# The start of a hybrid attention layer put in another order: modulation weights first, then the first head on half of the input

## The chip, the cores and the metric

The kernel runs on one core of a Trainium2 chip. The metric is the device time of one execution in microseconds (us). Five engines work beside each other, each through its own queue in order: TensorE (PE, matmuls; PEld is its weight load), VectorE (DVE), ScalarE (ACT), GpSimd (POOL) and SyncE (SP, which here issues every DMA).

## The reference

One layer of a diffusion backbone, for 1024 latent tokens and 256 context tokens of 1024 channels, in float32. What matters here is how it starts:

```python
shift_x, scale_x, gate_x = jnp.split(jax.nn.silu(c) @ w_mod[l] + b_mod[l], 3, axis=-1)
shift_c, scale_c, gate_c = jnp.split(jax.nn.silu(c_ctx) @ w_mod[l] + b_mod[l], 3, axis=-1)
hc = rmsnorm(ctx, norm_g[l]) * (1.0 + scale_c) + shift_c
...
_, s_f, s_b = gla_bidir(qc, kc, vc, laf_c, lab_c, s_zero, s_zero, not last)
hx = rmsnorm(x, norm_g[l]) * (1.0 + scale_x) + shift_x
q, k, v, la_f, la_b, zA, uB, zB, gA, gB = mixer_inputs(hx, w_in[l], ...)
ox, _, _ = gla_bidir(q, k, v, la_f, la_b, s_f, s_b, True)
```

The conditioning vectors give a shift and a scale for every channel. Each token row is normalised, scaled and shifted; that gives `h`. Then `h` is multiplied by the columns of `w_in`: queries, keys (4 heads of 128) and values (4 heads of 256), low-rank decay inputs, and the columns of the pooling branch and of the gates. The context gives the start states of the latent scans of all heads, so the gated linear attention of the first head waits for the context.

## The kernel before

**Numbers.** Every projection works on split floats: a float32 value is written as a high part (rounded to the matmul's `fp32r` format, by ScalarE) and a low part (the difference, by VectorE). `split` issues these two instructions. A product is then three `fp32r` matmuls (high·high, high·low, low·high), as in `proj_t` and `proj_n`.

**Modulation.** The loop over `b` in 0..3 (lines 211 to 243) makes shift and scale for both halves of the channels: b=0 is the shift of channels 0 to 511, b=1 their scale, b=2 and b=3 the same for channels 512 to 1023. For each it loads eight 256 KB pieces of `w_mod`. Pieces with an even index are multiplied as plain float32 (one `matmul` of the program, two on the engine); pieces with an odd index are split and multiplied as two `fp32r` matmuls. The stationary operand has only 4 columns. Then `mrow`, four small transposes (line 233) and two or three VectorE instructions give `shA` and `sA`.

**Token rows.** `load_x` and `normalise` bring in ten tiles of 128 tokens: tiles 0 and 1 are the context, 2 to 5 the first latent half, 6 to 9 the second. `split_rows` (line 184) takes one of eight channel blocks `kt` of a half: four transposes into a PSUM bank (`psc` for even kt, `ppj` for odd), then ScalarE and VectorE apply scale and shift and write the high and low part (`hH`, `hL`). `latent_rows(g, kts)` does this for latent half g, `context_rows` for the context. Channel blocks 0 to 3 need b=0 and b=1 only, blocks 4 to 7 need b=2 and b=3.

**Order.** Program order is: modulation b=0, b=1 with tiles 2 to 5 in between; `latent_rows(0, 0..3)`; low-rank weights (eight small loads for `wup`); modulation b=2, b=3 with tiles 0, 1, 6, 7, 8 in between, then tile 9; masks and rope tables; `latent_rows(0, 4..7)`; `low_rank(1)`; `context_rows`; `low_rank(0)`; `latent_rows(1)`; `low_rank(2)`; `ctx_gates` (decays of the context, all heads); and then the first head: `head_k`, `ctx_k`, `head_q`, `gates(0)`, `head_v`, `ctx_state(0)`. After these come the context states of heads 1 to 3 and `gla` for head 0. The rest (three more heads, pooling branch, gates, output) follows and is not touched.

**What sets the real order.** The program names tiles by a tag; a tag has a fixed number of buffers (`BUFS`, and `BANKS` for PSUM), and a new tile waits until the oldest one of its tag is released. A scheduler at build time lays out each engine's queue: it takes program order as the priority and may let an instruction that is ready pass one that waits. SP issues DMAs in its queue's order, and a load whose buffer isn't free holds up all that are behind it. Tags that matter here: `h` (32 buffers, modulation weights and then hH, hL), `wr` (2, raw weights), `wh`/`wl` (4 each, split weights), `bx` (1), `sw` (2), `pj` (3 banks), `sc` (2 banks), `tr`, `st` and `o` (1 bank each). `ctx_gates` and `gates` both use `bx`; `gates` and `ctx_state` both use the bank `tr`.

Of the kernel before, what the change touches and what calls it, by code (L numbers as in the profile page):

```python
# [10 lines left out]
F32R = mybir.dt.float32r  # L11
# [4 lines left out]
P = 128  # L16
D = 1024
KT = D // P
# [25 lines left out]
def hybrid_kernel(ctx: ExitStack, tc: tile.TileContext, x, ctx_in, rows, w_mod, b_gate_row,  # L44
# [83 lines left out]
    def load_x(t):  # L128
        tag = "S0" if t < 2 else "v" if t < 6 else "qk"
        loaded.append(t)  # L130
        src = ctx_in[t * P:(t + 1) * P] if t < 2 else x[(t - 2) * P:(t - 1) * P]
        xs[t] = [T(tag, [P, HALF]) for dh in range(2)]
        for dh in range(2):
            load(xs[t][dh], src[:, dh * HALF:(dh + 1) * HALF])
# [11 lines left out]
    def low_rank_weights():  # L146
        wraw = T("wr", [P, KT, 32])
        load(wraw, w_in[:, O_LR:O_LR + 32].rearrange("(k p) n -> p k n", p=P))
# [3 lines left out]
        for d in range(2):  # L152
            for part, srcw in enumerate((wlh, wll)):
                for rep in range(2):
                    act(wlr[:, :, d, part, rep, :], srcw[:, :, d * 16:(d + 1) * 16].bitcast(F32))
        wup = T("wr", [P, HALF])
        for rep in range(4):
            load(wup[rep * 16:(rep + 1) * 16], w_up_f)
            load(wup[64 + rep * 16:64 + (rep + 1) * 16], w_up_b)
        wup_hi, wup_lo = T("lr", [P, HALF], F32R), T("lr", [P, HALF], F32R)  # L160
# [23 lines left out]
    def split_rows(kt, t0, n, c, hi, lo):  # L184
        pt, sc_c, sh_c = modulate(kt, t0, n, c, ("sc", "pj")[kt % 2])
        hf = T("s2", [P, n])
# [21 lines left out]

    token_tiles = [2, 3, 4, 5, 0, 1, 6, 7, 8, 9]
    loaded = []  # L210
    for b in range(4):
        s_, half_ = b % 2, b // 2
        c0 = s_ * D + half_ * HALF
        pm = PT("st" if b % 2 else "tr")
        if b == 2:
            wlr, wup_hi, wup_lo = low_rank_weights()
        for kt in range(KT):
            w = T("h", [P, HALF])
            load(w, w_mod[kt * P:(kt + 1) * P, c0:c0 + HALF])
            if kt % 2 == 1 and token_tiles and b * KT + kt in (1, 3, 5, 7, 17, 19, 21, 23, 25, 27):  # L220
                load_x(token_tiles.pop(0))
                normalise(loaded[-1])
            if kt % 2 == 0:
# [5 lines left out]
            mm(pm[:4], cs4[:, kt, :], lo, False, kt == KT - 1)  # L229
        mrow = T("on", [4, HALF])  # L230
        act(mrow, pm[:4])
# [12 lines left out]

        if b == 1:
            latent_rows(0, range(4))
    for t in token_tiles:
        load_x(t)
    for t in token_tiles:
        normalise(t)  # L250

# [163 lines left out]

    def head_v(h, st):
        wv = weights_v(h)
        for t in range(8):
            if t % 2 == 0:
# [197 lines left out]

    msk_f = T("bx", [P, len(LEVELS) - 1, HC])
    load(msk_f, masks)
    nc.vector.tensor_copy(msk, msk_f)  # L620
    rope_t = T("t8", [P, 2, L])
    load(rope_t, rope)
    cosT, sinT = rope_t[:, 0, :], rope_t[:, 1, :]
    latent_rows(0, range(4, KT))
# [12 lines left out]
    ctx_state(0, kc, ctx_v(wv))  # L637
# [502 lines left out]
```

## Time and profile before

| | |
|---|---|
| median of 3 runs | 1144.55 us (1141.5 to 1146.18) |
| the profiled execution | 1143.17 us, of which the span is 1141.4 us |
| granted TensorE clock, mean | 0.996 |
| busy share of the span | PE 97%, PEld 79%, DVE 69%, ACT 44% |
| bytes moved | 138.21 MB, mean 121 GB/s |

The time of the profiled execution is its span and 1.8 us around it. Times in the rows are microseconds from the start of the span. A busy TensorE is one that has matmuls under way: since they are pipelined, it can count as busy while it waits inside a group, so the distance between starts says more than the length. The granted clock is a share of full speed: 1.00 is the level of 2.4 GHz, 0.5 that of 1.2 GHz, and a value between is a mean over the stretch.

### The profile page before, as it was taken

Reading aid. Unit: us, or ns where it says so; the run is one execution under the profiler, and the core shown is the slowest. Engines: PE = TensorE matmul, PEld = TensorE weight load, DVE = VectorE, ACT = ScalarE, POOL = GpSimd, SP = SyncE. Lnnn points to the kernel's source line nnn. Section 1 sums busy time; section 2 is a strip of 40 time slices with the busy share of each in tenths; the row PEclk is TensorE's granted clock in tenths of the full one; section 3 lists DMA queues with packets and bytes.
Section 4 is the critical chain, followed back from the end, with each engine's and each line's share of the span. In section 5 each row is a group of like instructions: output and inputs, shape, how many; then the busy total and the mean of one; then the engine's idle time right before and its main releaser. Section 6 shows DMA issues by size and latency. Waiting matters only on the chain.

```text
span 1141.4 us, 17328 instructions
## 1 busy us (share of the span) xinstructions
PE 1107.9 (97%) x6505; PEld 900.8 (79%) x6505; DVE 787.6 (69%) x1498; ACT 506.7 (44%) x994; POOL 25.5 (2%) x50
## 2 busy tenths in 40 slices
PE   6799999999999999999999999999999999999997
PEld 1268997797797787788888878888887787878997
DVE  4677458477487486798988977665657886647454
ACT  6687554464554543543333533343346422114233
POOL 0100000100100100100000000000000000000001
PEclk9899999999999999999999999999999999999999
DMA  8812150220210310113251664523239568962113
GB/s 293 286 38 74 50 150 24 63 67 20 76 55 20 93 38 20 56 31 121 97 162 42 203 194 129 162 84 126 91 122 313 199 194 304 307 222 93 38 38 148
DMA packets 119665, 138.21 MB, mean 121 GB/s; under 512 B 8803, under 2 KB 80797, under 8 KB 119454
## 3 DMA queue, kind: packets, MB, share of 16 engines
q1 hardware_dynamic: 119582, 137.12, 37.4%
q8 instruction: 51, 0.84, 0.3%
q14 instruction: 32, 0.26, 0.1%
HBM read 100.38 MB, written 32.51 MB: 116 GB/s over the span
## 4 chain that ended last, share of the span: by engine, by line
PE 85%; DMA 5%; ACT 4%; issue 2%; DVE 2%; SPq 1%; POOL 1%; POOLq 0%; ACTq 0%; DVEq 0%
PE ppj L78 60%; PE psc L78 17%; PE pst L78 3%; PE po L78 2%; PE ptr L78 2%; DMA h<-w_mod 1%; SPq L81 1%; ACT A L64 1%; POOL r L611 1%; ACT sw L64 1%; PE ptr L363 1%; DMA h<-ga 1%; DMA wr<-w_in 0%; ACT h L64 0%; DMA kt<-ga 0%
## 5 line engine op out<-in xcount | busy, mean ns | idle before, releaser
L78 PE MATMUL ppj<-h,wh 128*128 128x512 f32 x794 | 266.9, 404 | 1.1 <-DVE h L67 1.1
L64 ACT ACTIVATE wh<-wr 128x512 fp32r<-128x512 f32 (+1 forms) x183 | 113.8, 628 | 175.3 <-PE ppj L78 104.9
L78 PEld LDWEIGHTS ppj<-h,wh 128*128 128x128 f32 x794 | 148.0, 188 | 36.2 <-issue 2.0
L67 DVE TENSOR_TENSOR wl<-wr,wh 128x512 fp32r<-128x512 f32 (+1 forms) x183 | 124.4, 685 | 67.3 <-ACT wh L64 66.3
L78 PE MATMUL ppj<-wh,h 128*128 128x256 f32 x800 | 157.7, 283 | 0.0
L78 PE MATMUL ppj<-h,wl 128*128 128x512 f32 x397 | 157.1, 396 | 0.0
L78 PEld LDWEIGHTS ppj<-wh,h 128*128 128x128 f32 x800 | 130.5, 192 | 0.6 <-ACT qk L64 0.4
L78 PE MATMUL ppj<-wl,h 128*128 128x256 f32 x400 | 113.1, 283 | 0.0
L78 PEld LDWEIGHTS ppj<-h,wl 128*128 128x128 f32 x397 | 74.6, 188 | 15.2 <-issue 1.0
L78 PEld LDWEIGHTS ppj<-wl,h 128*128 128x128 f32 x400 | 76.6, 192 | 0.3 <-DVE wl L67 0.2
L75 DVE SCALAR_TENSOR_TENSOR S<-S,dec,pst 128x256 f32<-128x256 f32 x56 | 26.8, 479 | 42.5 <-PE pst L78 42.2
L64 ACT ACTIVATE s<-s 128x512 f32<-128x512 f32 x60 | 36.9, 629 | 35.8 <-DVE s L67 32.6
L67 DVE TENSOR_TENSOR s<-s,ppj 128x512 f32<-128x512 f32 x60 | 40.6, 681 | 15.5 <-PE ppj L78 15.5
L64 ACT ACTIVATE s<-qk 128x256 f32<-128x256 f32 x56 | 23.3, 425 | 47.4 <-DVE qk L67 47.3
L78 PE MATMUL ppj<-S,wh 128*128 128x512 f32 (+1 forms) x132 | 40.9, 371 | 0.0
L67 DVE TENSOR_TENSOR s<-s,psc 128x512 f32<-128x512 f32 x43 | 29.2, 682 | 16.0 <-PE psc L78 16.0
L78 PEld LDWEIGHTS psc<-z,s 128*64 128x64 f32 x768 | 26.4, 136 | 17.4 <-issue 14.5
L78 PE MATMUL psc<-h,wh 128*128 128x512 f32 x126 | 39.1, 392 | 0.0
L78 PE MATMUL pst<-v,kt 128*128 128x256 f32 x112 | 35.6, 399 | 0.0
L78 PE MATMUL ppj<-v,wh 128*128 128x512 f32 (+1 forms) x116 | 35.0, 360 | 0.0
L67 DVE TENSOR_TENSOR s<-s,bx 128x256 f32<-128x256 f32 (+1 forms) x64 | 30.3, 483 | 6.7 <-ACT bx L64 6.7
L64 ACT ACTIVATE qk<-wr 128x512 fp32r<-128x512 f32 x30 | 18.4, 626 | 35.9 <-DVE wr L67 21.2
(513 smaller groups left out, 2361.7 us busy)
## 6 DMA issues: line engine op xcount, KB each, us to landing
wr<-w_in SPq DMA_DIRECT2D x65, 512.0 KB, 3.7
h<-w_mod SPq DMA_DIRECT2D x32, 256.0 KB, 5.4
qk<-sg SPq DMA_DIRECT2D x32, 256.0 KB, 5.6
sg<-s SPq DMA_DIRECT2D x28, 256.0 KB, 2.1
sw<-qk SPq DMA_DIRECT2D x64, 64.0 KB, 2.0
gb_T<-qk SPq DMA_DIRECT2D x16, 256.0 KB, 2.8
qk<-o SPq DMA_DIRECT2D x16, 256.0 KB, 4.9
ga<-s SPq DMA_DIRECT2D x16, 256.0 KB, 3.9
```

The lines of the kernel that those rows point to most:

```text
L64: return nc.scalar.activation(out, in_, func, **kw)
L67: return nc.vector.tensor_tensor(out=out, in0=a, in1=b, op=op)
L75: return nc.vector.scalar_tensor_tensor(out=out, in0=a, scalar=s, in1=b, op0=op0, op1=op1)
L78: return nc.tensor.matmul(out, lhsT=lhsT, rhs=rhs, start=start, stop=stop)
L81: return nc.sync.dma_start(out=out, in_=in_)
L363: nc.tensor.transpose(pt[:, i * P:(i + 1) * P], src[i], ident)
L611: nc.gpsimd.tensor_tensor(out=r2[:, 2, :], in0=r2[:, 1, :], in1=mhalf.to_broadcast([P, 2]), op=ALU.pow)
```

## The change

The start is written in another order, and some of its parts change size or place.

- Modulation b=0 and b=1: six of eight pieces are now multiplied as plain float32 and two are split (before four and four). Tiles 2 to 5 are still loaded in between, at other places. b=2 and b=3 keep four and four.
- The key weights of head 0 are loaded right behind b=1, then the pieces of b=2, the query weights, and the pieces of b=3. The key weights get a tile `kbig` of tag `bx` for their split parts, the query weights four tiles of tag `s2`.
- Then follow the products of b=2 and b=3, the first half of the contraction of K and Q for token half 0 (`proj_part` with channel blocks 0 to 3), the low-rank weights, the loads of the context tiles and of tiles 6 to 9, `latent_rows(0, 4..7)`, the rest of K and Q for half 0, the loads of V's weights, rope and masks, the rotation of K and Q, the context tiles' norms, V for half 0, `context_rows`, `low_rank(1)`, the norms of tiles 6 to 9, `low_rank(0)`, `latent_rows(1)`, `ctx_k`, K for half 1, `low_rank(2)`, `ctx_gates`, Q for half 1, `gates(0)`, V for half 1, and `ctx_state(0)` as before.
- `split_rows` uses the two `sc` banks alone. The low-rank weights' raw tile goes to tag `A`, `wup` to `sw` and is loaded by two broadcast DMAs; tiles 6 to 9 go to `kt`, `qk`, `qk` and `S`; the masks' raw tile goes to `on`.

```diff
     def load_x(t):
-        tag = "S0" if t < 2 else "v" if t < 6 else "qk"
-        loaded.append(t)
+        tag = "S0" if t < 2 else "v" if t < 6 else ("kt", "qk", "qk", "S")[t - 6]
...
-        wup = T("wr", [P, HALF])
-        for rep in range(4):
-            load(wup[rep * 16:(rep + 1) * 16], w_up_f)
-            load(wup[64 + rep * 16:64 + (rep + 1) * 16], w_up_b)
+        wup = T("sw", [P, HALF])
+        for d, src in enumerate((w_up_f, w_up_b)):
+            load(wup[64 * d:64 * d + 64],
+                 src.rearrange("(a r) n -> a r n", a=1).to_broadcast([4, 16, HALF]))
...
-        pt, sc_c, sh_c = modulate(kt, t0, n, c, ("sc", "pj")[kt % 2])
+        pt, sc_c, sh_c = modulate(kt, t0, n, c, "sc")
...
+    def mod_part(b, pm, ws, kts):
+        for w, kt in zip(ws, kts):
+            if kt % (4, 2)[b // 2] != (3, 1)[b // 2]:
                 mm(pm[:4], sil4[:, kt, :], w, kt == 0, kt == KT - 1)
                 continue
             hi, lo = T("wh", [P, HALF], F32R), T("wl", [P, HALF], F32R)
             split(hi, lo, w)
             mm(pm[:4], cs4[:, kt, :], hi, kt == 0, False)
             mm(pm[:4], cs4[:, kt, :], lo, False, kt == KT - 1)
...
+    x_after = {(0, 3): 2, (0, 7): 3, (1, 1): 4, (1, 4): 5}
+    for b in range(2):
+        pm = PT("st" if b % 2 else "tr")
+        for kt in range(KT):
+            ws = mod_load(b, [kt])
+            if (b, kt) in x_after:
+                load_x(x_after[b, kt])
+                normalise(x_after[b, kt])
+            mod_part(b, pm, ws, [kt])
+        mod_finish(b, pm)
...
+    st = new_head()
+    kbig = T("bx", [P, 2, KT, P], F32R)
+    k_go = head_weights(O_K, [(kbig[:, 0, 4 * i:4 * i + 4], kbig[:, 1, 4 * i:4 * i + 4]) for i in range(2)])
+    ws2 = mod_load(2, range(KT))
+    q_go = head_weights(O_Q, [(T("s2", [P, 4, P], F32R), T("s2", [P, 4, P], F32R)) for i in range(2)])
+    ws3 = mod_load(3, range(KT))
+    latent_rows(0, range(4))
+    pm2, pm3 = PT("tr"), PT("st")
+    mod_part(2, pm2, ws2, range(KT))
+    mod_finish(2, pm2)
+    mod_part(3, pm3, ws3, range(KT))
+    mod_finish(3, pm3)
+    wk = k_go()
+    pk, pq = PT("pj"), PT("pj")
+    proj_part(pk, wk, 0, range(4))
+    wq = q_go()
+    proj_part(pq, wq, 0, range(4))
+    wlr, wup_hi, wup_lo = low_rank_weights()
+    for t in (0, 1, 6, 7, 8, 9):
+        load_x(t)
+    latent_rows(0, range(4, KT))
+    proj_part(pk, wk, 0, range(4, KT))
+    proj_part(pq, wq, 0, range(4, KT))
+    wv = weights_v(0)
...
+    st["k"][0] = rope_apply(pk, 0, 1.0)
+    st["q"][0] = rope_apply(pq, 0, float(P) ** -0.5)
+    for t in (0, 1):
+        normalise(t)
+    head_v(0, st, 0, wv)
+    context_rows()
     low_rank(1, hH[0], hL[0])
-    context_rows()
+    for t in (6, 7, 8, 9):
+        normalise(t)
     low_rank(0, hcH, hcL)
     latent_rows(1, range(0, KT))
+    kc = ctx_k(wk)
+    pk, pq = PT("pj"), PT("pj")
+    proj_part(pk, wk, 1, range(KT))
+    st["k"][1] = rope_apply(pk, 1, 1.0)
     low_rank(2, hH[1], hL[1])
     e_ctx = ctx_gates()
-    st = new_head()
-    wk = head_k(0, st)
-    kc = ctx_k(wk)
-    head_q(0, st)
+    proj_part(pq, wq, 1, range(KT))
+    st["q"][1] = rope_apply(pq, 1, float(P) ** -0.5)
     decays = gates(0)
-    wv = head_v(0, st)
+    head_v(0, st, 1, wv)
     ctx_state(0, kc, ctx_v(wv))
```

`head_weights` loads one weight slab into `wr` and returns a function that splits it into the tiles given; `proj_part` issues the three matmuls per channel block of `proj_t` for the blocks given, into a bank that stays open; `head_v` takes one token half and finished weights.

## Rows read from the trace of the kernel before

**Rows 1.** The page: busy time of each engine, and TensorE's busy tenths in 40 slices.

```profile
PE 1107.9 (97%) x6505; PEld 900.8 (79%) x6505; DVE 787.6 (69%) x1498; ACT 506.7 (44%) x994; POOL 25.5 (2%) x50
...
PE   6799999999999999999999999999999999999997
```

**Rows 2.** Eight stretches: length, busy of each engine, granted clock, DMA share, GB/s.

```profile
0.00:26.50 26.50, 18.50 (x61) 5.10 (x61) 11.57 (x34) 15.63 (x41) 2.53 (x9) 1.00 0.86 292
26.50:34.00 7.50, 5.17 (x20) 3.93 (x20) 5.65 (x11) 7.37 (x16) 0.55 (x1) 0.77 0.99 358
34.00:52.15 18.15, 13.53 (x41) 2.39 (x40) 11.30 (x32) 10.52 (x26) 2.74 (x5) 1.00 0.96 337
52.15:62.51 10.36, 7.68 (x30) 4.54 (x30) 8.54 (x18) 9.27 (x18) 0.00 (x0) 0.84 0.00 0
62.51:72.62 10.11, 9.39 (x58) 7.32 (x58) 9.74 (x19) 9.61 (x20) 0.00 (x0) 1.00 0.32 95
72.62:104.30 31.68, 31.56 (x146) 24.00 (x144) 22.20 (x46) 23.32 (x37) 0.20 (x2) 1.00 0.18 46
104.30:127.64 23.34, 23.34 (x194) 23.18 (x193) 14.91 (x49) 15.79 (x25) 0.00 (x0) 1.00 0.13 34
127.64:167.00 39.36, 39.36 (x306) 38.05 (x304) 18.65 (x31) 21.90 (x45) 0.00 (x0) 1.00 0.42 121
```

**Rows 3.** The chain of waits, in time: start, length, what.

```profile
25.83 5.92 DMA h<-w_mod
31.76 3.77 DMA qk<-x
```

**Rows 4.** SP's queue in time: start, length, what it issued.

```profile
37.85 2.36 SPq L81 DMA_DIRECT2D h<-w_mod  x4
...
42.36 28.00 SPq L81 DMA_DIRECT2D wr<-w_in  x4
```

**Rows 5.** TensorE in time: start, length of the merged instructions, what.

```profile
6.86 1.87 PE L78 MATMUL ptr<-h,sil 128*4 128x512 f32 x2 [2.95 <-ACT sil L64]
...
31.29 2.79 PE L78 MATMUL ppj<-h,z 128*128 128x512 f32 x7
...
38.00 0.39 PE L78 MATMUL ptr<-wh,cs 128*4 128x512 f32 x1
38.23 0.40 PE L78 MATMUL ptr<-wl,cs 128*4 128x512 f32 x1
38.56 1.02 PE L78 MATMUL ptr<-h,sil 128*4 128x512 f32 x2
39.51 0.40 PE L78 MATMUL ptr<-wh,cs 128*4 128x512 f32 x1
...
64.52 0.60 PE L177 MATMUL psc<-cst,qk 128*128 128x128 f32 x4
64.96 0.27 PE L177 MATMUL ppj<-cst,qk 128*128 128x128 f32 x1
...
92.18 0.63 PE L78 MATMUL ppj<-h,wh 128*128 128x512 f32 x2
...
102.86 0.39 PE L78 MATMUL ppj<-h,wl 128*128 128x512 f32 x1
```

**Rows 6.** Groups of instructions from 0 to 54 us: count, busy, mean ns.

```profile
L67 DVE TENSOR_TENSOR wl<-h,wh 128x512 fp32r<-128x512 f32 x16 | 10.7, 686 | 3.3 <-ACT wh L64 3.3
...
L64 ACT ACTIVATE wh<-h 128x512 fp32r<-128x512 f32 x16 | 9.6, 621 | 5.2 <-DMA h<-w_mod 5.2
```

**Rows 7.** DMA from 0 to 100 us, GB/s in 40 slices of 2.5 us.

```profile
GB/s 62 293 316 346 393 397 388 378 155 192 291 343 378 399 392 388 385 406 378 284 51 0 0 0 0 0 210 0 158 58 0 0 0 0 87 18 30 79 0 37
```

**Rows 8.** ScalarE in time, around the decay gates.

```profile
69.58 0.49 ACT L64 ACTIVATE z<-po,cols 128x256 f32<-128x256 f32 x1
...
97.27 0.50 ACT L64 ACTIVATE bx<-ptr,cols 128x256 f32<-128x256 f32 x1 [0.80 <-DVE z L326]
...
108.05 0.50 ACT L64 ACTIVATE bx<-ptr,cols 128x256 f32<-128x256 f32 x1 [0.28 <-DVE s L72]
```

More of the change, by code (lines that the diff above doesn't have):

```diff
@@ L146, in low_rank_weights @@
     def low_rank_weights():
-        wraw = T("wr", [P, KT, 32])
+        wraw = T("A", [P, KT, 32])
         load(wraw, w_in[:, O_LR:O_LR + 32].rearrange("(k p) n -> p k n", p=P))
@@ L207, in context_rows, with mod_load @@
             split_rows(kt, 0, LC, 1, hcH[kt], hcL[kt])
[L209 to L223, printed above, removed]
+    def mod_load(b, kts):
+        c0 = (b % 2) * D + (b // 2) * HALF
+        ws = []
+        for kt in kts:
+            ws.append(T("h", [P, HALF]))
+            load(ws[-1], w_mod[kt * P:(kt + 1) * P, c0:c0 + HALF])
+        return ws
+    def mod_part(b, pm, ws, kts):
+        for w, kt in zip(ws, kts):
+            if kt % (4, 2)[b // 2] != (3, 1)[b // 2]:
                 mm(pm[:4], sil4[:, kt, :], w, kt == 0, kt == KT - 1)
@@ L229, in hybrid_kernel, with mod_finish @@
             mm(pm[:4], cs4[:, kt, :], lo, False, kt == KT - 1)
+    def mod_finish(b, pm):
+        s_, half_ = b % 2, b // 2
         mrow = T("on", [4, HALF])
@@ L243, in hybrid_kernel @@
             tt(sA[:, ks, :], sA[:, ks, :], col4(cols[:, R_NG + half_ * 4:R_NG + half_ * 4 + 4]), ALU.mult)
[L245 to L250, printed above, removed]
+    x_after = {(0, 3): 2, (0, 7): 3, (1, 1): 4, (1, 4): 5}
[8 more added lines that the diff above has]
+        mod_finish(b, pm)
     ahead = [False]
@@ L414, in rope_apply, with head_v @@
         return q
-    def head_v(h, st):
-        wv = weights_v(h)
-        for t in range(8):
+    def head_v(h, st, hf=None, wv=None):
+        wv = wv or weights_v(h)
+        for t in range(8) if hf is None else range(hf * CPH, hf * CPH + CPH):
             if t % 2 == 0:
@@ L615, in gla, with head_weights, go, proj_part @@
                 load(o_dram[h][c0:c0 + 2].rearrange("c p n -> p c n"), on)
-    msk_f = T("bx", [P, len(LEVELS) - 1, HC])
-    load(msk_f, masks)
-    nc.vector.tensor_copy(msk, msk_f)
+    def head_weights(c0, tiles):
+        raw = T("wr", [P, KT, P])
+        load(raw, wcols(w_in, c0))
+        def go():
+            for i in range(2):
+                split(*tiles[i], raw[:, 4 * i:4 * i + 4, :])
+            return [tuple(t[:, k, :] for t in tiles[i]) for i in range(2) for k in range(4)]
+        return go
+    def proj_part(pt, w, hf, kts):
+        for k in kts:
+            whi, wlo = w[k]
+            mm(pt, whi, hH[hf][k], k == 0, False)
+            mm(pt, whi, hL[hf][k], False, False)
+            mm(pt, wlo, hH[hf][k], False, k == KT - 1)
+    st = new_head()
[22 more added lines that the diff above has]
+    wv = weights_v(0)
     rope_t = T("t8", [P, 2, L])
@@ L623, in hybrid_kernel @@
     cosT, sinT = rope_t[:, 0, :], rope_t[:, 1, :]
-    latent_rows(0, range(4, KT))
+    msk_f = T("on", [P, len(LEVELS) - 1, HC])
+    load(msk_f, masks)
+    nc.vector.tensor_copy(msk, msk_f)
+    st["k"][0] = rope_apply(pk, 0, 1.0)
[4 more added lines that the diff above has]
+    context_rows()
     low_rank(1, hH[0], hL[0])
-    context_rows()
+    for t in (6, 7, 8, 9):
+        normalise(t)
     low_rank(0, hcH, hcL)
     latent_rows(1, range(0, KT))
+    kc = ctx_k(wk)
+    pk, pq = PT("pj"), PT("pj")
+    proj_part(pk, wk, 1, range(KT))
+    st["k"][1] = rope_apply(pk, 1, 1.0)
     low_rank(2, hH[1], hL[1])
     e_ctx = ctx_gates()
-    st = new_head()
-    wk = head_k(0, st)
-    kc = ctx_k(wk)
-    head_q(0, st)
+    proj_part(pq, wq, 1, range(KT))
+    st["q"][1] = rope_apply(pq, 1, float(P) ** -0.5)
     decays = gates(0)
-    wv = head_v(0, st)
+    head_v(0, st, 1, wv)
     ctx_state(0, kc, ctx_v(wv))
```

## Prediction

> **What bounds the kernel now.** I read the page first. TensorE is busy for 97% of the span, and of its 40 slices the first shows 6 tenths, the second 7, the last 7, and all others 9 [rows 1]. So only work that closes a hole of TensorE can shorten the kernel, and the large holes lie in the first two slices, some 57 us. What comes later starts when the start is over, so a microsecond won here should last to the end.
>
> Then I cut the start into stretches [rows 2]. The cuts are: scale of the lower channels ready (26.5), last modulation products begin (34), scale of the upper channels ready (52.15), context rows under way, first matmul of K (72.6), end of K and Q (104.3), end of V of head 0 (127.64), context states, about the start of head 0's attention (167). From 72.6 on TensorE is full. Before that three limits follow each other. Up to 52 us it is data: DMA is at 0.86 to 0.99 and the chain of waits runs through a modulation piece and a token tile that share the queue [rows 3]; the last pieces are issued only at 37.85 to 40.2 [rows 4]. From 52 to 72.6 ScalarE and VectorE bind: 18.9 and 18.3 of 20.5 us busy, while TensorE waits for rows. Meanwhile DMA has nothing to do. All projections of the first head wait behind both limits, though half of their input could be ready.
>
> **How full the start is.** I add up what TensorE must do before V of head 0 ends, by distances between starts [rows 5]: a plain float32 modulation piece costs 0.95 us (38.56 to 39.51), a split one 0.56 (38.00 to 38.56); a transpose 0.11 (four from 64.52 to 64.96); a matmul of 512 columns 0.227 (48 from 92.18 to 102.86); one of 256 columns 0.12 (V, some 192 in 23.34 us [rows 2]).
>
> **The change, part by part.**
>
> *Modulation b=0, b=1.* 12 plain pieces and 4 split ones: 12 x 0.95 + 4 x 0.56 = 13.6 us. The first three pieces run at the slow level as the first does now (1.87 for its two matmuls against 1.02 later): 2.6 more. With only two banks, 8 transposes can be done ahead: 0.9. From 6.86 that gives 24.0, and 24.4 with the small transposes (an estimate of 0.4 for each b). Today's end is about the same. Four pieces that are no longer split cost TensorE 4 x 0.39 = 1.6 us and spare ScalarE 2.5 and VectorE 2.7 [rows 6]; I count the first and take the second as hidden.
>
> *Modulation b=2, b=3.* Loads: 32 pieces, tiles 2 to 5, the weights of K and Q and the constants are 8.4 + 2.1 + 1.05 + 0.2 = 11.7 MB. The first eight DMA slices carry 6.4 MB by 20 us; 5.3 MB more at 390 GB/s land at 33.6 [rows 7]. TensorE needs 8 x 0.95 + 8 x 0.56 = 12.1, transposes 0.9 and 0.8 of small ones: 24.4 + 13.8 = 38.2, so it is TensorE, no longer the DMA, that sets this end. ScalarE has in the same 13 us eight splits (5.0), four of K and Q (2.5) [rows 6] and the first four row blocks (under 5, for all its work from 26.5 to 34 is 7.4 [rows 2]). It is nearly full, so I add 1.5 for late splits: 39.7. Today the scale is there at 52.15.
>
> *What is left for TensorE then.* K and Q of head 0: 96 x 0.227 = 21.8. V: 23.3. Low rank: 32 x 0.227 + 16 x 0.12 = 9.2. Context K: 24 x 0.12 = 2.9. Transposes: 64 x 0.11 = 7.0. Decay gates: 16 x 0.12 + 16 x 0.227 = 5.6. Sum 69.8: without any wait V ends at 39.7 + 69.8 = 109.5 against 127.64, which is 18.1 us earlier.
>
> *Does the work come in time?* K and Q over blocks 0 to 3 (48 x 0.227 / 2 = 5.4) cover the making of blocks 4 to 7. V for half 0 (11.7) covers the context. The loads moved behind b=3 (low-rank weights, 3.1 MB of tiles, 1 MB for V) land by about 33.6 + 4.6 / 0.39 = 45.4; V starts near 51, so 5 us hide the splits of its weights. Without that cover each late microsecond counts in full. Rows of half 1: ScalarE has been busy 55 us when they end today, by the stretches up to 72.6 and 3 more. In the new order its sum up to there is about 57 (less 2.5 for pieces, less 1.4 for gates that come later, plus 2.5 for V's weights, 1.2 for the rotation, 1.5 for V's results), and about 29 of that falls before 41. The other 28 at 95% end at 71. TensorE wants the last row at 39.7 + 43.5 = 83 (its work up to the end of K for half 1), so there are 12 us of slack. I take 3.5 us for waits where single rows come late (between 0 and the 12 that two thirds of today's pace would cost), 1 for starting matmuls at the slow level, and 1 for the bank below.
>
> *Moved past queues, at nothing.* SP issues two broadcasts for `wup` instead of eight loads (now in the slices at 155 and 192 GB/s); what waits for them is the decay gates at 80 us or later, so even several microseconds stay hidden. Rope and masks come with V's weights, some 40 us before the attention. The masks wait in SP's queue for `on`, which the last `mrow` frees near 41; behind them are only the rotation's copies, due after 51. `low_rank(1)` waits for both `sw` buffers until the rotation is done (near 60) and stands behind V anyway.
>
> *Sum.* 18.1 - 3.5 - 1 - 1 = 12.6 us. 1143.17 - 12.6 = 1130.5. The profiled execution is 1.4 us under the median of the runs shown, which is within their spread; I leave it there. The best case is no wait and no late split: 127.64 - 38.2 - 69.8 = 19.6, so 1123.5.
>
> **The clock.** In the stretches from 26.5 and from 52.15, each after a hole of TensorE, the granted clock is 0.77 and 0.84, and seven matmuls of 512 columns take 2.79 us instead of 1.6; from 34 to 52, with TensorE 75% busy, it is 1.00 [rows 2, 5]. The Trainium skill, "TensorE: Matmul & The Clock Gate", Part 1, says that the slow level is the resting state and that activity lifts it; the trace agrees where it shows 0.77. By that page, longer starvation would cost double; that is the rival on the slower side.
>
> **The rivals.**
>
> *Row blocks and splits stay late.* From 34 to 52 ScalarE and VectorE were only 58 and 62% busy, since each waits for the other. At that pace the 12.5 us of ScalarE's work after 26 take 21, modulation ends at 47, and V at 47 + 69.8 + 4.5 = 121.3: 6.3 us gained, 1137. Against it: today they waited for data, which will have landed. The two `sc` banks speak for it. The Trainium skill, "Perfetto Trace Analysis", Matmuls, says that independent groups should rotate through different PSUM banks, and the change cuts them from five to two; no row shows two.
>
> *The gates come late.* `ctx_gates` needs `bx`, which `kbig` holds until K for half 1 is done, near 86 with waits. Today 27.7 us pass from the first context gate to the first use of `bx` by `gates(0)`, and 11.3 more until the bank `tr` is read last [rows 8]. That would be 125, while `ctx_state(0)` wants `tr` at 114 + 5.8 = 119.8. A stall of 5 instead of 1: 1134.5. Against it: those 27.7 us ran beside a ScalarE that was 90% busy, and the scheduler has context K of head 1 to put in between. Attention itself is due near 154, after the gates' end.
>
> *Slower: the clock falls.* Between 39.7 and 83 TensorE has 43.5 us of work. If starvation in it pulls the mean clock to 0.65, it takes 67 and V ends at 133: 5.3 us later than now, 1148. It decides from a mean of 0.70 downwards (43.5 / 0.70 - 43.5 = 18.6). The lowest mean of any stretch is 0.77.
>
> **How the numbers follow.** The forecast, 1130.5 with its own range 1125 to 1136, gets 0.57; late rows (1136 to 1141) 0.18; late gates 0.17; the clock 0.08. Half a percent, 5.7 us, is about what can be told from no change: the bound is 1137.5. Faster: 0.55 + 0.05 + 0.14 = 0.74. Slower: 0.07. The same: 0.19. The range from 1124 to 1142 leaves out the clock and the ends of the others.
>
> **What would show it.** In the profile after, the scale of the upper channels should be ready near 41 instead of 52; K matmuls should stand before it; DMA should stay near 390 GB/s to about 45 without the dip at 20 to 25; V of head 0 should start near 51 and end near 114, with the context states' 39.4 us unchanged behind it. I am wrong if TensorE shows holes between 41 and 86, if the chain runs through `sc` banks or `bx`, or if the granted clock there is below 0.9.

## The result, and the profile after

The changed kernel takes 1136.13 us in the median of 6 runs (1135.06 to 1138.38); the kernel before, beside it, 1143.31 us (1141.5 to 1146.18, 6 runs). The ratio is 0.9935, with a 95% interval from 0.9921 to 0.995. So 7.2 us are gone, where 12.6 were forecast: the time lies in the range given, and 0.1 us beyond the upper end of the forecast's own range. The profiled execution took 1136.27 us, with a span of 1134.5.

The page after, against [rows 1]: TensorE does the same number of instructions in nearly the same busy time, and the first two of 40 slices have 7 and 9 tenths instead of 6 and 7.

```profile
PE 1104.8 (97%) x6505; PEld 899.1 (79%) x6505; DVE 785.8 (69%) x1494; ACT 504.4 (44%) x990; POOL 25.5 (2%) x50
...
PE   7999899999999999999999999999999999999997
```

The fifth digit is an 8 where before it was a 9: a new hole at 113 to 142 us. The same eight stretches as in [rows 2] say more (length, busy of PE, PEld, DVE, ACT, POOL, granted clock, DMA share, GB/s):

```profile
0.00:26.50 26.50, 20.07 (x54) 4.22 (x55) 10.60 (x32) 13.55 (x31) 2.53 (x9) 1.00 0.96 333
26.50:34.00 7.50, 6.76 (x22) 1.18 (x22) 3.29 (x7) 3.40 (x6) 0.00 (x0) 1.00 1.08 364
34.00:52.15 18.15, 16.96 (x78) 10.19 (x76) 13.78 (x31) 17.15 (x42) 1.64 (x3) 1.00 1.01 299
52.15:62.51 10.36, 9.91 (x72) 9.29 (x73) 7.52 (x20) 8.29 (x21) 1.61 (x3) 1.00 0.66 199
62.51:72.62 10.11, 10.11 (x73) 9.22 (x72) 8.53 (x19) 5.08 (x12) 0.03 (x1) 1.00 0.06 14
72.62:104.30 31.68, 30.79 (x181) 24.97 (x179) 16.62 (x29) 19.82 (x32) 0.10 (x1) 1.00 0.04 9
104.30:127.64 23.34, 20.66 (x156) 18.96 (x156) 17.29 (x41) 19.77 (x32) 0.10 (x1) 1.00 0.16 41
127.64:167.00 39.36, 37.75 (x334) 34.31 (x334) 28.00 (x69) 26.44 (x53) 0.00 (x0) 1.00 0.45 131
```

From 34 to 104 TensorE is now nearly full (78 instructions instead of 41 from 34 to 52), and the clock is 1.00 in all eight stretches; before, 0.77 stood from 26.5 to 34 and 0.84 from 52 to 62.5. But the last two stretches, which were full (23.34 and 39.36 us busy), now have 2.7 and 1.6 us of holes, with ScalarE at 19.8 and 26.4 us instead of 15.8 and 21.9.

Four marks in time carry the comparison. In the kernel before they stand here (start, length, what): upper scale ready, first split of the context weights of head 1 on ScalarE, first VectorE instruction of attention in heads 0 and 1. V of head 0 ends at 127.64, the cut of [rows 2].

```profile
52.55 0.17 DVE L67 TENSOR_TENSOR sA<-sA,cols 128x8 f32<-128x8 f32 x1
...
131.44 2.79 ACT L64 ACTIVATE wh<-wr 128x512 fp32r<-128x512 f32 x4 [0.34 <-PE ppj L78]
...
170.41 0.69 DVE L75 SCALAR_TENSOR_TENSOR lr<-psc,id 128x512 f32<-128x512 f32 x1 [2.37 <-PE psc L78]
252.47 0.68 DVE L75 SCALAR_TENSOR_TENSOR lr<-psc,id 128x512 f32<-128x512 f32 x1
```

And after, with the first matmul of context V of head 0, which is the end of head 0's own V:

```profile
42.45 0.17 DVE L67 TENSOR_TENSOR sA<-sA,cols 128x8 f32<-128x8 f32 x1
...
115.03 0.28 PE L78 MATMUL ppj<-wh,S 128*128 128x256 f32 x1
...
162.72 0.69 DVE L75 SCALAR_TENSOR_TENSOR lr<-psc,id 128x512 f32<-128x512 f32 x1 [2.32 <-PE psc L78]
244.77 0.68 DVE L75 SCALAR_TENSOR_TENSOR lr<-psc,id 128x512 f32<-128x512 f32 x1
```

V of head 0 ends 12.61 us earlier (127.64 to 115.03). That equals the forecast's 12.6 only by chance: the forecast had the end near 114 and took 1 us off behind it. Attention begins only 7.69 us earlier (170.41 to 162.72), and 7.70 at head 1. So 4.92 us were won and lost again between the two: this way took 42.77 us before and takes 47.69 now, for the same 356 instructions of TensorE (before, then after):

```profile
127.64:170.41 42.77, 42.77 (x356) 40.87 (x356) 19.69 (x33) 23.23 (x48) 0.00 (x0) 1.00 0.44 127
115.03:162.72 47.69, 43.85 (x356) 40.81 (x356) 32.08 (x79) 35.85 (x67) 0.00 (x0) 1.00 0.40 113
```

What TensorE waits for from 100 to 165 says where (engine, line, waited for: total us, times, longest; the same view of the kernel before has no row from 127 to 165):

```profile
PE pst L78 <- ACT on L64: 1.6, 2, 1.2
PE ppj L78 <- ACT wh L64: 1.3, 1, 1.3
PE po L78 <- DVE bx L72: 1.2, 2, 1.0
PE ppj L78 <- DVE wl L67: 0.6, 2, 0.3
PE ptr L366 <- DVE kt L67: 0.3, 1, 0.3
```

Except for the third row, which lies before V's end, these are instructions of the context states: split weights `wh` and `wl`, and the transposed result `on`. They come to 3.8 us, which is the 3.84 us that TensorE is idle on this way. The other 1.1 us are no gaps: the same instructions are busy for 43.85 us instead of 42.77. ScalarE in time shows what stood in front of them:

```profile
118.76 0.49 ACT L64 ACTIVATE bx<-po,cols 128x256 f32<-128x256 f32 x1
119.54 0.49 ACT L64 ACTIVATE bx<-ptr,cols 128x256 f32<-128x256 f32 x1 [0.29 <-DVE s L72]
119.93 0.36 ACT L64 ACTIVATE S<-ppj 128x256 f32<-128x256 f32 x1
120.19 1.91 ACT L64 ACTIVATE bx<-bx 128x2048 f32<-128x2048 f32 x1
121.99 2.18 ACT L64 ACTIVATE wh<-wr 128x512 fp32r<-128x512 f32 x4
124.19 1.28 ACT L64 ACT_TABLE_LOAD   x1
125.48 1.91 ACT L64 ACTIVATE bx<-bx 128x2048 f32<-128x2048 f32 x1
127.30 0.36 ACT L64 ACTIVATE S<-ppj 128x256 f32<-128x256 f32 x1
127.56 0.59 ACT L64 ACTIVATE on<-ptr 128x512 f32<-128x512 f32 x1
```

The weights' splits came 3.80 us after V's end before (131.44), and 6.96 us after it now (121.99): eight gate instructions on `bx` and the 1.91 us Exp of `gates(0)` go first. The table load and the Ln then hold up `S` and `on`. Before, the same gate work ran beside V ([rows 8]: first at 97.27, 30 us ahead of V's end); now its first instruction on `bx` is at 116.23.

### The profile page after: what moved, and what is told of

Its sections match the earlier page's. It is cut to its first block, busy times and chain, and to the rows that moved or that the text cites. A ratio compares the mean times of both kernels' runs of the same rounds, so it can differ in the third digit from the quotient of the medians.

```text
span 1134.5 us, 17289 instructions
## 1 busy us (share of the span) xinstructions
PE 1104.8 (97%) x6505; PEld 899.1 (79%) x6505; DVE 785.8 (69%) x1494; ACT 504.4 (44%) x990; POOL 25.5 (2%) x50
## 4 chain that ended last, share of the span: by engine, by line
PE 84%; ACT 5%; DMA 5%; DVE 3%; issue 2%; POOL 1%; SPq 1%; POOLq 0%; ACTq 0%; DVEq 0%
PE ppj L78 58%; PE psc L78 17%; PE pst L78 3%; PE po L78 2%; PE ptr L78 1%; DMA h<-w_mod 1%; DMA wr<-w_in 1%; ACT A L64 1%; POOL r L614 1%; ACT bx L64 1%; SPq L81 1%; DMA kt<-ga 1%; PE psc L176 1%; ACT wh L64 1%; ACT L64 1%
## 5 line engine op out<-in xcount | busy, mean ns | idle before, releaser
L78 PE MATMUL ppj<-h,wh 128*128 128x512 f32 x730 | 245.8, 405 | 0.0
L64 ACT ACTIVATE wh<-wr 128x512 fp32r<-128x512 f32 x178 | 110.1, 628 | 171.7 <-PE ppj L78 102.9
L78 PEld LDWEIGHTS ppj<-h,wh 128*128 128x128 f32 x730 | 136.3, 188 | 32.1 <-issue 1.9
L67 DVE TENSOR_TENSOR wl<-wr,wh 128x512 fp32r<-128x512 f32 x178 | 120.7, 686 | 53.0 <-ACT wh L64 50.4
L78 PE MATMUL ppj<-h,wl 128*128 128x512 f32 x365 | 144.7, 397 | 0.0
L78 PEld LDWEIGHTS ppj<-h,wl 128*128 128x128 f32 x365 | 68.7, 188 | 13.7 <-issue 1.0
L67 DVE TENSOR_TENSOR s<-s,ppj 128x512 f32<-128x512 f32 x60 | 40.6, 682 | 15.9 <-PE ppj L78 15.8
L78 PEld LDWEIGHTS psc<-z,s 128*64 128x64 f32 x768 | 26.4, 136 | 17.4 <-issue 14.5
L78 PE MATMUL ppj<-S,wh 128*128 128x512 f32 (+1 forms) x124 | 38.6, 376 | 1.3 <-ACT wh L64 1.3
L78 PE MATMUL psc<-z,s 128*64 128x64 f32 x768 | 33.0, 227 | 0.0
```

The source lines that it names most:

```text
L64: return nc.scalar.activation(out, in_, func, **kw)
L67: return nc.vector.tensor_tensor(out=out, in0=a, in1=b, op=op)
L78: return nc.tensor.matmul(out, lhsT=lhsT, rhs=rhs, start=start, stop=stop)
```

## The experiments

All were timed in five rounds beside the kernel before, whose medians were 1144.2 to 1145.5 us in these jobs; the ratio is the number to compare. Marks in us from the start of each profiled span:

| kernel | median us | ratio [95%] | scale ready | V of head 0 ends | attention, head 0 | head 1 |
|---|---|---|---|---|---|---|
| before | 1143.31 | | 52.55 | 127.64 | 170.41 | 252.47 |
| after | 1136.13 | 0.9935 [0.9921, 0.995] | 42.45 | 115.03 | 162.72 | 244.77 |
| e1, own tiles for context gates | 1137.32 | 0.9936 [0.9922, 0.9949] | 43.59 | 115.83 | 162.62 | 244.69 |
| e2, and context gates earlier | 1137.47 | 0.994 [0.9928, 0.9952] | 43.13 | 119.14 | 163.51 | 245.60 |
| e3, gates behind context state 1 | 1134.61 | 0.991 [0.9898, 0.9923] | 42.73 | 112.69 | 159.75 | 242.16 |
| e4, modulation first alone | 1146.44 | 1.001 [1.0, 1.002] | 40.40 | 128.26 | 170.78 | 252.85 |
| e5, four split and four plain | 1137.99 | 0.9946 [0.9927, 0.9965] | 43.83 | 116.13 | 164.07 | 246.13 |
| e6, five banks | 1137.07 | 0.9934 [0.9917, 0.9952] | 43.02 | 115.42 | 163.63 | 245.66 |
| e7, eight loads for `wup` | 1139.78 | 0.9961 [0.9947, 0.9975] | 42.66 | 117.43 | 165.32 | 247.39 |
| e8, e4 with five banks | 1146.88 | 1.0019 [1.0007, 1.0032] | 40.26 | 129.03 | 171.63 | 253.68 |
| e9, no Exp and Ln in `gates(0)` | 1135.17 | 0.9907 [0.9887, 0.9927] | 42.38 | 114.95 | 159.73 | 241.77 |
| e10, gates before Q of half 1 | 1138.06 | 0.9933 [0.9914, 0.9952] | 42.70 | 114.73 | 159.87 | 244.03 |
| e11, gates behind context state 0 | 1134.25 | 0.9902 [0.9881, 0.9922] | 43.19 | 113.15 | 160.20 | 242.26 |
| e12, e11 and low rank later | 1134.43 | 0.9903 [0.9882, 0.9925] | 41.09 | 112.26 | 159.53 | 241.59 |

Each row of marks is of one execution. Eight of these kernels have the same program up to the upper scale (the changed one, e1 to e3, e7, e9 to e11), and their scale is ready between 42.38 and 43.59. So a single mark that differs by about 1 us shows nothing.

### Where the five microseconds went: the gates

**e1, the link through `bx`.** The context gates get tiles of their own, so `bx` goes from `kbig` straight to `gates(0)`. If the tag `bx` is what makes the gates late, this should give the loss back.

```diff
-        xm = T("bx", [P, 2, 2, 2, LC])
-        xm = [xm[:, i] for i in range(2)]
+        xm = [T("S0", [P, 2, LC]) for _ in range(NH)]
```

> The changed kernel ends V of head 0 12.6 us earlier than the kernel before (115.0 against 127.6), but keeps only 6.9 us of it in its span: the stretch from there to the attention takes 44.3 us against 39.4. Theory A: one chain costs this. The buffer bx is held by K's split weights until K for half 1 is done, then by the context gates, and only then comes gates(0), whose long ScalarE instructions now stand between the weight splits and copies that the context states wait for. Here the context gates' second operand lies in four tiles of tag S0, so that bx goes from K's weights straight to gates(0), and nothing else changes. Theory A: first use of bx by gates(0) 10 us or more earlier than 116, the holes of TensorE at 121 and 127 (1.3 and 1.2 us) gone, 41 us or less from V's end to the attention, 1132 to 1134. Theory B, the rival: the stretch is tight by itself, since head 1's weights can be split only when V's split weights are released and ScalarE must do that in 4 us in any case: the holes stay, 1135 to 1137.

The first instruction on `bx` moved from 116.23 to 104.50, but the last one of the gates only from 144.04 to 143.12, and attention from 162.72 to 162.62. The median is that of the changed kernel within the interval. TensorE's longest wait, for `wh`, was still there (1.6 us, against 1.3). The handover of `bx` is not what costs the time.

**e2, context gates earlier.** e1, and `ctx_gates` right behind `low_rank(0)`, so that nothing of the context's decays is left when the latent gates come.

```diff
     low_rank(0, hcH, hcL)
+    e_ctx = ctx_gates()
     latent_rows(1, range(0, KT))
...
-    e_ctx = ctx_gates()
```

> As the kernel with the context gates' own tiles, and ctx_gates also stands right behind low_rank(0), ahead of the rows of half 1, as far as the buffers z let it. Theory A: the two context gates' tiles no longer meet gates(0) and V on ScalarE, 40 us or less from V's end to the attention, 1130 to 1133. Theory B: 1135 to 1137. A third possibility: the gates now stand in front of the rows of half 1 on ScalarE and VectorE, the last row comes later than 84.6, and K for half 1 waits: 1136 to 1140.

The way from V's end to attention shrank from 47.69 to 44.37 us, but V's end moved 4.1 us back, to 119.14: the context gates' work on ScalarE and VectorE now stood in front of the rows of half 1 and the low-rank results, and TensorE waited there (2.0 us for `lr`, 0.8 for `h`). The same loss in another place, and nothing won.

**e3, gates later.** `gates(0)` is taken from ahead of V's second half and put behind the context state of head 1, where TensorE has work of its own and attention isn't due yet.

```diff
-    decays = gates(0)
     head_v(0, st, 1, wv)
...
         ctx_state(h, ctx_k(weights_k(h)), ctx_v(weights_v(h)))
+        if h == 1:
+            decays = gates(0)
```

> The changed kernel with gates(0) moved behind the context state of head 1, all else as it is. Theory A: the holes at 121 and 127 go, since the splits of head 1's weights come first; but the gates took 28 us from 116 to 144 and now start near 130, so that they end near 158 and the attention, due at about 155, waits 3 us or a little more: 1134 to 1138, with the wait now ahead of the attention instead of in the context states. Theory B: the holes stay where they are and the late gates come on top: 1138 to 1141.

V ends at 112.69, 2.34 us earlier: the gates' eight matmuls (8 x 0.227 = 1.8 us) now stand behind it, and the waits for `bx` in front of it shrink from 1.2 us to 0.2. The splits of the context weights start at 116.44, 3.75 us after V's end, as in the kernel before, and the 1.3 us wait for `wh` is down to 0.4. Attention begins 2.97 us earlier than in the changed kernel, and the ratio is 0.991. Without the 1.8 us of gate matmuls, the way from V's end to attention is 47.06 - 1.8 = 45.3 us instead of 47.69. The last gate instruction is at 161.16, just after attention's first.

**e9, the price of the two large activations.** The place of the gates stays that of the changed kernel, but `gates(0)` leaves out the Exp and the Ln over 2048 columns.

```diff
-        act(both, both, AF.Exp, scale=-1.0)
-        act(both, both, AF.Ln, bias=1.0)
+        if full:
+            act(both, both, AF.Exp, scale=-1.0)
+            act(both, both, AF.Ln, bias=1.0)
```

> The changed kernel, with the two large activations (Exp and Ln over 2048 columns) of the first head's gates left out, so its decays are not the reference's. They are 1.91 and 1.91 us, and two table loads of 1.28 us stand with them: some 6.4 us of ScalarE between 120.2 and 129.7, where TensorE then shows holes of 1.33 and 1.23 us before split weights and on. Theory (ScalarE's gate work behind the end of V costs the 5 us): the way from the end of V (115.0) to the first instruction of attention shrinks from 47.7 to 43 to 45 us and the median falls by 3 to 5 us, to 1131 to 1133. Rival (weights of the context heads arrive late by DMA, or VectorE's gate work): it stays at 46.5 to 47.7 and the median within 1 us of 1136.1.

V ends at the same time (114.95), and the way from there to attention is 44.78 us instead of 47.69: 2.9 of the 4.9 us hang on these two instructions and the two table loads beside them. The head 1 mark agrees (241.77, 3.00 earlier). The ratio to the kernel before fell by 0.0028; the median alone fell by less, by 1.0 us, which is within the spread of the runs. The remaining 2 us stayed, and here the waits are for `on` (1.0 us) and no longer for `wh`.

**e10, more cover in front.** With e1's tiles, `gates(0)` is put before Q of half 1, so more of TensorE's work lies behind it. It is Q of half 1, which is 24 x 0.227 = 5.4 us, and half of V; the 10.9 in the expectation is Q of both halves.

```diff
+    decays = gates(0)
     proj_part(pq, wq, 1, range(KT))
     st["q"][1] = rope_apply(pq, 1, float(P) ** -0.5)
-    decays = gates(0)
```

> The changed kernel with the gates of the first head put before Q of token half 1 instead of behind it, and with e1's own tiles for the context gates so that they need not wait for bx. Theory (the change left only half of V, 11.7 us, behind the gates to cover them, where the kernel before had all of V, 23.3 us): with Q's 10.9 us as more cover the last gate instruction moves from 144 to about 133, the way from V's end to attention falls from 47.7 to 43 to 45, and the median to 1131 to 1134. Rival (gates are held by what they need, the low-rank rows of half 1 and the context gates, not by where they stand, as in e1): the way stays at 46 or more and the median within 1 us of 1136.1.

A miss. The large Exp came only 2.6 us earlier (117.61 instead of 120.19) and the Ln 4.4 us (121.10), so both now stood back to back in front of the context weights' splits, which began at 122.92. What holds the gates here is the work of ScalarE and VectorE that stands before them, that of the context gates above all: ScalarE is busy for 13.0 of the 14 us from 98 to 112, and VectorE for all 6 from 112 to 118. (The scheduler pulled the first scores of head 0 ahead, so head 0's mark says nothing here; by head 1's, 0.74 us were won, which is within the scatter.) TensorE had one hole where the changed kernel has several, and the granted clock fell behind it. In stretches of 2 us (columns as in the eight stretches):

```profile
118.00:120.00 2.00, 2.00 (x19) 2.00 (x18) 1.62 (x4) 1.98 (x3) 0.00 (x0) 1.00 0.00 0
120.00:122.00 2.00, 1.01 (x9) 0.77 (x8) 0.00 (x0) 1.99 (x2) 0.00 (x0) 1.00 0.03 8
122.00:124.00 2.00, 0.41 (x2) 0.42 (x2) 0.96 (x2) 2.00 (x4) 0.00 (x0) 0.90 0.00 0
124.00:126.00 2.00, 2.00 (x10) 1.66 (x10) 2.00 (x4) 1.98 (x6) 0.00 (x0) 0.50 0.00 0
126.00:128.00 2.00, 2.00 (x12) 1.92 (x12) 2.00 (x6) 1.56 (x2) 0.00 (x0) 0.74 0.90 248
```

From 120 to 124 TensorE is busy for 1.42 of 4 us while ScalarE is full (3.99), and then the clock stands at 0.50, which is the level of 1.2 GHz, for a whole stretch.

**e11, gates behind the context state of head 0.** The place between the changed kernel's and e3's.

```diff
-    decays = gates(0)
     head_v(0, st, 1, wv)
     ctx_state(0, kc, ctx_v(wv))
+    decays = gates(0)
```

> The changed kernel with the gates of the first head right behind the context state of head 0, between the kernel given (before V's second half) and e3 (behind the context state of head 1: 1134.6). Theory: all places behind V are alike so long as the gates end before attention (about 160); median 1134 to 1135.5, attention starts 2 to 3 us earlier than 162.72. Rival: what counts is the distance from the context gates' own ScalarE work (107 to 115), so this place is no better than the given one: 1136 to 1137.

The ratio is 0.9902, attention begins 2.52 us earlier than in the changed kernel, and the gates are finished at 150.27, ten microseconds ahead of attention. So the place need not be exact; it must only not be in front of the first context splits. What TensorE still waits for from 100 to 165:

```profile
PE ppj L78 <- DVE wl L67: 0.6, 1, 0.6
PE ppj L78 <- ACT wh L64: 0.6, 1, 0.6
PE ptr L366 <- DVE kt L67: 0.5, 1, 0.5
PE po L78 <- DVE bx L72: 0.2, 1, 0.2
PE pst L78 <- ACT on L64: 0.2, 1, 0.2
```

That is 2.1 us instead of 5.0.

### Where the twelve microseconds came from

**e4, modulation first alone.** The loads and splits of all four modulation blocks come first with the new tiles, banks and splits, and behind them stands the old order: all rows, then K, Q and V of head 0 over both halves. The early loads of the key and query weights and the half-first order are left out.

> One part of the change alone: the modulation weights come first, with their splits, banks and tile places as changed, and then the old order: all rows, low rank, context gates, and K, Q and V of head 0 on full token halves behind them. By the sums of the prediction the scale of the upper channels is ready near 42 as in the changed kernel, but from there to the last row TensorE has only low rank and transposes to do, and the rows of half 1 end when ScalarE is through, near 68 to 71 against 76.4 before: 5 to 8 us won at the front, nothing lost in the context states since bx and the gates come early: 1136 to 1139. Rival: the half-first order is what wins, and this part alone gives under 3 us: 1140 to 1143. Other rival: the half-first order costs what it wins, and this part alone gives more than the whole: 1131 to 1134.

None of the three expectations has this: the median is above the kernel before. The upper scale is ready at 40.40, 12 us earlier than in the kernel before, and V of head 0 ends at 128.26, 0.6 later. The stretches show why, against [rows 2]:

```profile
34.00:52.15 18.15, 13.57 (x61) 7.20 (x59) 14.03 (x33) 15.96 (x41) 1.65 (x3) 0.95 0.89 288
52.15:62.51 10.36, 8.62 (x34) 6.23 (x34) 8.36 (x25) 9.39 (x26) 2.08 (x3) 0.66 0.00 0
62.51:72.62 10.11, 9.41 (x40) 6.96 (x41) 8.01 (x14) 7.11 (x14) 0.00 (x0) 0.76 0.36 104
```

After the modulation ScalarE and VectorE make rows for everything, TensorE has little but transposes and low-rank groups to do, and its clock falls to 0.66 and 0.76. K begins early, at 65.18 instead of 72.62, but the transposes of the last rows come at 75.2 instead of 69.8. From 72.6 on the counts are those of the kernel before (146 and 191 instructions in the next two stretches; before 146 and 194): all that was won at 40 us is gone by then. So it takes what e4 leaves out, the half-first order with its early weights, which gives TensorE K, Q and V of half 0 in this time, to turn the early scale into a gain. The half-first order without the early modulation was not run; what it gives alone is open.

**e8, e4 with five banks.** Row blocks use `sc` and `pj` in turn again, to see whether the two banks held e4's rows back.

```diff
-        pt, sc_c, sh_c = modulate(kt, t0, n, c, "sc")
+        pt, sc_c, sh_c = modulate(kt, t0, n, c, ("sc", "pj")[kt % 2])
```

> The kernel with modulation first and the old order behind it (e4, 1146.4), but with five banks for the row blocks. If the two banks ate what e4 won (scale ready 10 us earlier), V of head 0 ends 5 to 10 us before e4's 128.26 and the median falls to 1137 to 1141. If it is ScalarE and VectorE, which still have all rows to make before K, V ends within 1.5 us of 128.26 and the median stays within 1.5 us of 1146.4.

1146.88 against 1146.44, V's end at 129.03: no gain. The banks are not what held e4.

**e6, five banks in the changed kernel.** The same edit there.

> The changed kernel, but the row blocks alternate between the tags sc and pj again (five banks instead of two). The prediction charged the two banks 1 to 3.5 us of late rows. If that is right, V of head 0 ends at 112 to 114 (changed kernel 115.03) and the median falls by 1 to 3 us. Rival: K and Q hold two of the three pj banks open, so a row block waits for pj instead and V ends at 115 or later; median within 1 us of 1136.1 or above.

V ends at 115.42, 0.4 us later, and the ratio is the same. No cost of the two banks shows.

**e5, four split and four plain pieces in b=0 and b=1.**

```diff
-            if kt % (4, 2)[b // 2] != (3, 1)[b // 2]:
+            if kt % 2 == 0:
```

> The changed kernel, but the first two modulation blocks keep four plain and four split pieces as before. If TensorE sets their end, as the prediction counts, 1.6 us of plain products go away: V of head 0 ends near 113.5 (changed kernel 115.03) and the median falls to about 1134.6. Rival: ScalarE and VectorE set it (2.5 and 2.7 us more of splits there): V ends near 117 and the median is about 1138.5.

The time goes the rival's way: the scale is ready 1.38 us later, V ends 1.10 later, attention begins 1.35 later. But the reason is another, and it stands at the first product (the changed kernel, then e5):

```profile
4.68 5.28 PE L78 MATMUL ptr<-h,sil 128*4 128x512 f32 x6 [0.73 <-ACT cs L64]
...
6.95 1.87 PE L78 MATMUL ptr<-h,sil 128*4 128x512 f32 x2 [3.04 <-ACT sil L64]
```

`sil` is the operand of the plain products. Where the second piece is split, as in e5 and the kernel before, ScalarE takes that split first and makes `sil` only at 6.70 (6.60 in the kernel before); in the changed kernel the fourth piece is the first to be split, and `sil` is made at 4.27. From the first product to the small transposes of b=1, TensorE takes 18.85 us in e5 and 20.03 in the changed kernel (19.1 to 21.1 in all kernels with six plain pieces). So plain pieces do cost TensorE time, 1.2 us here, and the start, 2.27 us sooner, pays for it. With marks that scatter by 1.2 us and ratios whose intervals overlap, it is not settled which of the two is faster.

**e7, eight loads for `wup` again.**

```diff
-        for d, src in enumerate((w_up_f, w_up_b)):
-            load(wup[64 * d:64 * d + 64],
-                 src.rearrange("(a r) n -> a r n", a=1).to_broadcast([4, 16, HALF]))
+        for rep in range(4):
+            load(wup[rep * 16:(rep + 1) * 16], w_up_f)
+            load(wup[64 + rep * 16:64 + (rep + 1) * 16], w_up_b)
```

> The changed kernel, but wup comes by eight small loads again instead of two broadcasts. Hidden, as the prediction counts: V of head 0 ends within 0.5 us of 115.03, median within 1 us of 1136.1, only the DMA rate of the slices behind it moves. Rival: eight loads that take few DMA engines hold up V's weights and the context tiles in SP's queue, and V of head 0 ends 2 us or more later.

Attention begins 2.60 us later and the median is 3.65 us higher. DMA from 30 to 70 us, GB/s in 40 slices of 1 us, in e7:

```profile
GB/s 385 381 387 387 339 220 90 49 29 92 367 219 244 289 326 367 399 406 389 369 349 363 407 434 229 0 0 0 0 0 83 325 185 255 362 231 163 46 31 115
```

and in the changed kernel:

```profile
GB/s 373 391 393 389 294 214 221 221 227 248 340 350 303 371 283 322 224 250 316 375 367 432 391 191 73 12 140 331 219 311 249 173 43 74 57 0 0 0 0 0
```

With eight loads the rate falls to 29 to 92 GB/s from 36 to 40; with two broadcasts it stays at 214 or above. SP's queue says why (the changed kernel's first three rows, then e7's first and last load of `wup` and what follows):

```profile
31.64 0.69 SPq L81 DMA_DIRECT2D sw<-w_up_f  x1
32.38 0.55 SPq L81 DMA_DIRECT2D sw<-w_up_b  x1
32.99 2.37 SPq L81 DMA_DIRECT2D S<-ctx  x4
...
31.84 0.51 SPq L81 DMA_DIRECT2D sw<-w_up_f  x1
...
36.87 1.30 SPq L81 DMA_DIRECT2D sw<-w_up_b  x1
38.21 2.04 SPq L81 DMA_DIRECT2D S<-ctx  x4
```

In e7 the eight loads of 32 KB each stand in it from 31.84 to 38.17, most of them 0.67 us apart, and the context tiles behind them are issued at 38.21; in the changed kernel two issues take from 31.64 to 32.93, and the tiles follow at 32.99. All that follows in the queue lands later, and ScalarE begins to split V's weights at 57.23 instead of 51.39; TensorE waits 1.3 us for them at 57.9, which it doesn't in the changed kernel, and V of head 0 ends 2.40 us later.

### A further version: e11 with the low-rank weights later

**e12, low-rank weights later.** e11, with `low_rank_weights()` moved from ahead of row blocks 4 to 7 to just ahead of V's weights.

> e11 (gates behind the context state of head 0; 1134.25) with the low-rank weights taken from ahead of the row blocks 4 to 7 to just ahead of V's weights. In the changed kernel ScalarE makes the low-rank copies and splits from 40.5 to 43.1 while TensorE then waits for single rows (0.4 to 0.5 us each, four times, from 46 to 54). If that order costs the rows, the holes between 46 and 54 shrink, V of head 0 ends 1 to 2 us before e11's 113.15, and the median is 1132 to 1133.5. Rival: the splits now stand ahead of V's weights and the loads ahead of V's in the queue, so V starts as late or later; V ends at 113 to 115 and the median is 1134 to 1136.

The scale is ready 2.1 us earlier than in e11, but V's end is only 0.9 earlier and attention 0.7, both within the scatter, since a single wait of 1.6 us for a row (VectorE's `s`) takes most of it back. The expected 1 to 2 us at V's end are not shown. The medians of e11 and e12 can't be told apart (1134.25 and 1134.43). e3, e11 and e12 are each about 0.3 percentage points below the changed kernel in ratio; their intervals overlap with its own, but the marks at heads 0 and 1 agree that 2.5 to 3.2 us are gone.

## Why the prediction was right, and by how much it was off

The direction and the mechanism of the gain were right, and the time lies in the range. The size was off by 5.6 us (1130.5 forecast), and one step has most of it: "the context states' 39.4 us unchanged behind it", together with the 1 us allowed "for the bank". The way from V's end to attention grew by 4.92 us instead of 1, which is 3.9 us. V's end itself is 1.0 us later than "near 114", and the last 0.8 us are lost between attention's start and the end of the span, which is within the spread of the runs. Part of the fit is luck, as the step by step account shows:

**Modulation b=0, b=1.** Forecast 24.4 with the small transposes; those of b=1 are at 24.71. That the end held is luck: the forecast counts from a first product at 6.86, as before, and it came at 4.68, because ScalarE now makes `sil` ahead of the first split, which the forecast did not see. From there to b=1's small transposes it took 20.0 us where 17.5 were counted. The cost of four more plain pieces, 1.6 us, is near the 1.2 that e5 shows.

**Modulation b=2, b=3.** Forecast 39.7 for the products, 41 for the scale; the last product ends at 39.4, and the scale is ready at 42.45. The small transposes of b=3 were issued at 41.13, behind eight matmuls of K that TensorE had taken meanwhile. K stood before the scale, as forecast, and DMA kept 323 to 397 GB/s from 7.5 to 35 us, without the dip of [rows 7] at 20 to 25:

```profile
GB/s 59 273 314 381 397 392 390 379 323 389 374 330 384 352 219 234 331 328 265 330 405 177 123 282 181 57 0 0 0 0 0 7 0 0 0 79 26 0 0 0
```

It did not stay near 390 to 45, as I had written: from 35 to 40 it is 219 and 234.

**The rest of TensorE's work.** 69.8 us, 3.5 of waits, 1 at the slow level and 1 for the bank were forecast from the products' end to V's end, 75.3 in all. From 39.4 to 115.03 it is 75.6 us. The agreement hides two errors. The waits listed in it are 0.6 + 0.5 + 0.4 us from 40 to 60 and 1.2 from 100 on, 2.7 together, nearly all of the 3.0 us that TensorE is idle there; the slow level didn't occur. So TensorE is busy for 72.7 us, 2.9 more than the sum. And the sum is itself 1.8 us too long: it counts 16 matmuls of 512 columns for the decay gates, where the program and the trace have eight. Its prices by distances between starts, or work that it leaves out, are therefore 4.7 us short in all; which is open. V's first matmul is at 52.80, and from 55.8 on they follow each other without a gap (forecast: near 51); V ends at 115.03 where "near 114" stood.

**`wup` and the queues, "at nothing".** The broadcasts were costed by who waits for `wup`, and hidden. e7 shows that the way of loading it is worth 2.6 us at attention, through what stands behind it in SP's queue. The forecast didn't miss by it, since the sum was made for the change with the broadcasts in it; but the reason given, that even several microseconds would stay hidden, was wrong.

**The rivals.** *Late rows and two banks* (1137): the time fits, the mechanism doesn't. Waits for rows from 40 to 60 are 1.5 us, and with five banks (e6) nothing is won. The rule cited there of the Trainium skill, "Perfetto Trace Analysis", Matmuls, to rotate independent groups through banks, is not contradicted by this; no run here shows a gain from more than two. *Late gates* (1134.5): this is what happened, in the right place, at 4.9 instead of 5 us, but not through the link named. The buffer `bx` and the bank `tr` were blamed; e1 removes the wait for `bx` and changes nothing, and the transposes of the first context state, which need `tr`, stand at 120.71 right behind context V. What costs the time is that the gates' work on ScalarE comes in front of the context weights' splits: e3 and e11 give back 3.0 and 2.5 us by moving it, e9 2.9 by leaving two instructions out. Why it comes so late is argued, not shown: from the transposes of the last rows to V's end 57.8 us passed before (69.80 to 127.64) and 33.2 pass now (81.82 to 115.03), since half of V stands in front of them; e10, with 5.4 us more behind the gates, brought the large Exp only 2.6 us forward. Some 2 to 2.5 us of the way stay in all three (44.78 in e9, 45.3 in e3 and in e11 without the gates' matmuls, against 42.77 before), and which of the other instructions on ScalarE and VectorE holds them is open. Two of the forecast's own signs of being wrong appeared: TensorE is idle for 1.7 us between 41 and 86, less than the 3.5 allowed, and the chain of waits runs through instructions on `bx`, first the context gates' and then those of `gates(0)`, with others between, from 102.67 to 127.4. *The clock* (1148): not in the changed kernel, but e4, with 0.66 and 0.76, shows that it was no invention. There TensorE issues 34 and 40 instructions in the stretches of 10 us where the changed kernel issues 72 and 73. That bears out what the Trainium skill, "TensorE: Matmul & The Clock Gate", Part 1, says of the resting level.

## What to carry to other kernels

When work is taken forward out of a stretch that was full, ask what else ran beside it: the cover of every other engine's work there goes with it. Here V's first half went to the front, and the decay gates, which had run under it unseen, came to stand before the next stage's weight splits; moving them one stage back cost one line and gave some 2.5 us. And loading earlier is worth nothing by itself (e4): what counts is whether TensorE has work for the time that it frees.

## What the runs showed of the hardware

Which kernel loses the clock could not be read from TensorE's busy time in stretches of 5 us. From 120 to 125 it was busy for 4.05 us in e1 and for only 3.44 in the changed kernel; then, from 125 to 130, e1's granted clock was 0.66 and the changed kernel's 1.00. What TensorE did just before tells more. Its longest hole in e1 was 1.58 us, until 125.93, and in e10 2.58 us, until 123.59, with 0.50 from 124 to 126 behind it. The changed kernel had two holes, of 1.33 us until 122.66 and of 1.23 until 128.20, and kept 1.00.

In these rows the number of loads in SP's queue counts for more than their size: most of the eight 32 KB loads of `wup` stood 0.67 us apart in e7, and four context loads of 256 KB took 2.04 us behind them, 0.51 each.

Exp and Ln of the gates cost two table loads of 1.28 us, one before the Ln and one behind it. The Trainium skill, "ScalarE: Activation LUTs", section "Table sets: the hidden batching unit", names a set that has both functions. The trace here shows a load between Exp and Ln and another behind Ln, so this program doesn't use it. What it would spare of ScalarE is, as an estimate from the rows, up to 2.56 us per gate; no run here tried it.
